# The first stage of a two-layer encoder step, ordered by columns of x instead of by k tiles

## The chip, the cores and the metric

The kernel runs on one core of a Trainium2 chip. The metric is the device time of one execution in microseconds (us). Three runs of the kernel before gave 1068.53, 1067.67 and 1068.82 us, median 1068.53. The kernel is given once with its profile; all times "at" some microsecond below count from the first instruction of the profiled execution. In the text TensorE is also called PE, VectorE DVE, ScalarE ACT, GpSimd POOL and SyncE SP, as the profile names them.

## What is computed

Two layers run over 1024 prompt rows and 64 sample rows (1088 columns in the kernel, which holds everything with features on the partitions). Each layer modulates a normalised input and multiplies it with a wide weight:

```python
cs = jax.nn.silu(c)
for l in range(DEPTH):
    shift, scale, gate = jnp.split(cs @ ada_w[l] + ada_b[l], 3, axis=-1)
    h = _rmsnorm(x, norm_g[l]) * (1 + scale[:, None]) + shift[:, None]
    ... h @ w_in ...
    x = x + gate[:, None] * out
```

This case concerns only the start of layer 0: load x, `h = x * rstd * A + B` with `A = norm_g * (1 + scale)` and `B = shift`, and the first two of the weight tiles of `h @ w_in`. All of it is float32 with exact products: h and each weight are split into a rounded high part and a low rest, and three products (high x high, high x low weight, low h x high weight) are summed.

## The kernel before

x arrives as 8 k tiles of 128 features by 1088 columns. The columns form three chunks (`CHUNKS`: 364, 364 and 360 columns; the last has the prompt's end and all 64 sample columns, so its two parts take different modulation columns). `startup` (L304) does this, with the order of each engine's instructions written out by hand from L367 on (`manual_schedule`: each engine's queue is the program's order):

- SP issues the loads in program order (L308 to L324): 8 tiles of x whole, unit 0 of the modulation weight (2 MiB), k tiles 0 and 1 of two weight tiles W0 and W1, unit 1, their k tiles 2 to 7, units 2 and 3.
- Squares on ScalarE (L329) and their sum over k tiles on VectorE (L331, in `acc`), then per chunk three products with ones on TensorE (`sums`, L383), a power -1/2 on GpSimd (L387), a broadcast by transposes (L395), and a copy back to `acc` by ScalarE (L396): `acc` then holds rstd for every column.
- `ada_steps` (L166 to L184) makes the shift and scale of two k tiles from one unit: 64 records of products on TensorE, a copy of the rows by VectorE (`ada_rows`, L170), a transpose (L173), additions (L179) and A (L184). Unit u gives k tiles 2u and 2u+1. `unit(u)` issues the products and the copy, the rest comes where `all_of(steps)` stands.
- `scale` (L347) multiplies a k tile of x by rstd on VectorE. `h` (L349) then makes two passes of ScalarE (L357): the rounded high part `ah` and the unrounded value `hf`, each in two pieces (prompt and sample columns); VectorE makes `al = hf - ah` (L364).
- `w_split` (L403) makes the high part of the weights on ScalarE (L405) and the low part by a subtraction on GpSimd, or for k tiles 2 to 7 of W1 on VectorE (L407).
- `part(kt, ns, which)` (L334) issues one to three of the products of k tile kt for both weight tiles and all three chunks: 6 products for each of the three kinds, 144 in all, into six PSUM banks `first` that stay open to the end of the stage.

After the stage the six banks are evacuated (L1013), one more modulation unit runs on TensorE and the products of all further weight tiles follow (L269 and others).

## Time and profile before

| | us |
|---|---|
| median of three runs | 1068.53 |
| the profiled execution | 1068.52 |
| span of its instructions | 1066.8 |
| TensorE busy in the span | 1043.7 |
| first product of the stage starts | 26.61 |
| last products of the stage start | 57.25 and after |

The span is the time from the first to the last instruction of the profile; 1.7 us lie around it. A row of the timeline gives start, length, engine, line, operation and tiles (written<-read), shapes and a count; in square brackets stand the idle time of the engine before it and what ended that. Matmuls overlap: six that start 0.167 us apart show as 1.16 us. Windows give busy time of each engine and the granted clock of TensorE (1.00 is 2.4 GHz, 0.50 is 1.2 GHz).

### The profile page before, as it was taken

What the parts mean: (1) busy time and instruction counts of PE and PEld (TensorE: products, weight loads), DVE (VectorE), ACT (ScalarE), POOL (GpSimd) and SP (SyncE); (2) the same over time, 40 slices, a digit from 0 to 9 for tenths busy, and PEclk for the clock granted to TensorE, in tenths of its full rate; (3) what the DMA queues carried; (4) which work ended last, traced back from release to release, by engine and by line L of the source; (5) the groups of instructions that cost most, each with busy time, mean ns of one, the idle gap of its engine ahead of it and who ended that gap; (6) DMA issues with size and microseconds to landing.
All of it is one profiled execution on the core that took longest, in us unless ns stands there. A gap on an engine that the chain in (4) does not pass through costs nothing.

```text
span 1066.8 us, 20069 instructions
## 1 busy us (share of the span) xinstructions
PE 1043.7 (98%) x7535; PEld 1014.4 (95%) x7535; DVE 722.3 (68%) x1854; ACT 591.7 (55%) x1160; POOL 498.9 (47%) x531
## 2 busy tenths in 40 slices
PE   6999999999999999999999999999999999999996
PEld 5999889999999999999999999999999999998996
DVE  5723889888887767677786455885478666776134
ACT  5935776856776697677687233643345343355110
POOL 1124313465576365455366356564346444465221
PEclk9999999999999999999999999999999999999998
DMA  9862521211010120000001712031111311124012
GB/s 362 339 240 96 213 99 61 82 57 43 22 40 25 40 75 21 21 21 19 3 20 42 266 69 100 40 120 40 41 41 31 129 41 60 60 80 158 1 69 99
DMA packets 31008, 90.30 MB, mean 85 GB/s; under 512 B 5568, under 2 KB 11968, under 8 KB 27456
## 3 DMA queue, kind: packets, MB, share of 16 engines
q1 hardware_dynamic: 30912, 89.03, 23.7%
q8 instruction: 59, 0.97, 0.4%
q14 instruction: 37, 0.30, 0.1%
HBM read 78.44 MB, written 10.58 MB: 83 GB/s over the span
## 4 chain that ended last, share of the span: by engine, by line
PE 90%; DVE 4%; ACT 2%; issue 2%; POOL 1%; DMA 0%; POOLq 0%; DVEq 0%; ACTq 0%
PE st L1393 21%; PE pj L269 19%; PE op L269 16%; PE pj L286 14%; PE av L793 3%; PE logit_ps L749 3%; PE p_ps L775 3%; PE ada_ps L167 2%; PE first L342 2%; PE score_ps L485 2%; PE sgu_ps L1461 1%; PE score_ps L486 1%; DVE acc L331 1%; POOL x L1281 1%; PE v_ps L1433 1%
## 5 line engine op out<-in xcount | busy, mean ns | idle before, releaser
L259 POOL TENSOR_TENSOR w_lo<-w_raw,w_hi 128x1024 fp32r<-128x1024 f32 x35 | 84.3, 2408 | 147.2 <-ACT w_hi L258 140.8
L269 PE MATMUL pj<-ah,w_hi 128*128 128x364 f32 (+1 forms) x440 | 145.2, 330 | 0.0
L269 PE MATMUL pj<-al,w_hi 128*128 128x364 f32 (+1 forms) x440 | 144.6, 329 | 0.0
L269 PE MATMUL pj<-ah,w_lo 128*128 128x364 f32 (+1 forms) x440 | 143.3, 329 | 0.0
L1393 PE MATMUL st<-ah,p_w 128*128 128x272 f32 x704 | 137.3, 290 | 0.3 <-ACT ring L1494 0.3
L604 DVE TENSOR_SCALAR_CACHE_REDUCE junk<-S,cand 128x512 bf16<-128x512 f32 (+5 forms) x142 | 119.0, 838 | 2.2
L1393 PEld LDWEIGHTS st<-ah,p_w 128*128 128x128 f32 x704 | 111.7, 188 | 1.4 <-issue 0.7
L286 PE MATMUL pj<-ah,w_lo 128*128 128x364 f32 (+1 forms) x304 | 100.3, 330 | 0.0
L286 PE MATMUL pj<-ah,w_hi 128*128 128x364 f32 (+1 forms) x304 | 100.2, 330 | 0.0
L286 PE MATMUL pj<-al,w_hi 128*128 128x364 f32 (+1 forms) x304 | 100.1, 329 | 0.0
L1360 POOL TENSOR_TENSOR p_w<-p_s,p_w 128x512 fp32r<-128x512 f32 x44 | 58.7, 1337 | 79.4 <-ACT p_w L1359 79.3
L1393 PE MATMUL st<-al,p_w 128*128 128x272 f32 x352 | 93.0, 291 | 0.0
L631 ACT ACTIVATE junk<-S,cand 128x896 bf16<-128x896 f32 (+2 forms) x78 | 77.7, 997 | 26.4 <-DVE m L634 24.5
L1253 DVE SCALAR_TENSOR_TENSOR x<-op,mod,x 128x192 f32<-128x192 f32 (+2 forms) x64 | 30.1, 495 | 91.4 <-PE op L269 87.5
L269 PEld LDWEIGHTS pj<-ah,w_hi 128*128 128x128 f32 x440 | 82.6, 188 | 0.6 <-ACT w_hi L258 0.3
L269 PE MATMUL op<-ah,w 128*128 128x448 f32 (+2 forms) x336 | 82.5, 330 | 0.4 <-DVE u L1420 0.4
L756 POOL TENSOR_SCALAR S<-S,sm 128x128 f32<-128x128 f32 (+8 forms) x68 | 51.6, 763 | 66.6 <-DVE sm L755 55.0
L269 PEld LDWEIGHTS pj<-al,w_hi 128*128 128x128 f32 x440 | 82.7, 188 | 0.1
L269 PEld LDWEIGHTS pj<-ah,w_lo 128*128 128x128 f32 x440 | 82.5, 188 | 0.0
L1393 PEld LDWEIGHTS st<-al,p_w 128*128 128x128 f32 x352 | 66.3, 188 | 0.3 <-issue 0.2
L269 PE MATMUL op<-ah,w_hi 128*128 128x384 f32 (+2 forms) x200 | 65.2, 326 | 0.0
L269 PE MATMUL op<-ah,w_lo 128*128 128x384 f32 (+2 forms) x200 | 65.1, 326 | 0.0
(322 smaller groups left out, 2977.1 us busy)
## 6 DMA issues: line engine op xcount, KB each, us to landing
ada<-in_ada_w SPq DMA_DIRECT2D x21, 1024.0 KB, 7.6
w_raw<-in_w SPq DMA_DIRECT2D x31, 512.0 KB, 3.5
p_raw<-in_w SPq DMA_DIRECT2D x44, 256.0 KB, 2.9
w_raw<-in_wo SPq DMA_DIRECT2D x16, 512.0 KB, 3.5
x<-in_x SPq DMA_DIRECT2D x8, 544.0 KB, 6.0
bo<-in_ada_w SPq DMA_DIRECT2D x2, 1024.0 KB, 6.9
x<-in_x SPq DMA_DIRECT2D x1, 1792.0 KB, 7.6
spill<-x SPq DMA_DIRECT2D x1, 1792.0 KB, 5.7
```

What stands on the lines that cost most here:

```text
L259: (nc.gpsimd if lo_eng == "pool" else nc.vector).tensor_sub(lo, raw, hi)
L269: last = self.nc.tensor.matmul(ps, wt[:, kt, :], at[:, kt, c0:c1], start=n == 0, stop=n == len(mms) - 1)
L286: self.nc.tensor.matmul(ps, wt[:, kt, :], at[:, kt, a:b], start=kt == 0 and i == 0, stop=kt == KT - 1 and i == 2)
L604: V.tensor_scalar(junks[0][:, 0:SW[j]], self.S[:, span(j)], thr, 0.0, op0=OP.is_lt, op1=OP.add, accum_out=col(cv, j))
L631: nc.scalar.activation(junks[1][:, 0:SW[j]], self.S[:, span(j)], AF.Sign, scale=-1.0, bias=col(cand, j), accum_out=col(cv, j))
L749: nc.tensor.matmul(pt[:, 0:w], lhs, keys[i][:, t // 2, s], start=i == 0, stop=i == 1)
L756: self.lastnorm = nc.gpsimd.tensor_scalar(p, p, st[:, 3:4], 0.5, op0=OP.mult, op1=OP.mult).ins
L775: nc.tensor.transpose(pt[0:r, o:o + P], p[:, j * P:j * P + r], self.ident)
L793: self.lastav = nc.tensor.matmul(av[:, 0:m], self.vs[0:r, vbase + j, t // 2, :], part[0:r, x:x + m], start=j == 0 and i == 0, stop=(j + 1) ...
L1253: nc.vector.scalar_tensor_tensor(x[:, t, a:b], ps[:, a:b], self.mod[l][:, 16 + t, j:j + 1], x[:, t, a:b], op0=OP.mult, op1=OP.add)
L1360: nc.gpsimd.tensor_sub(w[:, 1], src, w[:, 0])
L1393: nc.tensor.matmul(ps, w[:, p, k, :], at[:, k, :], start=i == 0, stop=i == len(mms) - 1)
```

## The change

The first stage goes by columns. `C2` is 728, the start of the last chunk. "Front" means columns 0 to 727, "back" 728 to 1087.

- Loads: columns 0 to 727 of all k tiles of x, unit 0, k tiles 0 to 3 of W0 and W1, unit 1, columns 728 to 1087 of all k tiles of x, unit 2, k tiles 4 to 7 of W0 and W1, unit 3. That is 8 loads more.
- Squares, sums and rstd are made for the front first, and for the back later, between other work. The bank `last` takes the sums and the rstd of the back.
- `part` takes the chunks as well, and the products of k tiles 0 to 3 are issued front and back separately. k tiles 4 to 7 are made whole, as before.
- `h` takes one k tile and its spans. For an even k tile it is as before. For an odd one VectorE first does `x = x * A * acc` (scalar_tensor_tensor in the place of `scale`), ScalarE makes `ah = x + B` in one pass, and VectorE makes `al = (x + B) - ah` (scalar_tensor_tensor in the place of the subtraction).
- `w_split` takes both weight tiles, k tiles 0 and 1, then 2 and 3, then 4 to 7; all low parts go to GpSimd.

```diff
         for kt in range(KT):
-            self.load(x[kt], self.i["x"][:, kt, :])
+            self.load(x[kt][:, 0:C2], self.i["x"][:, kt, 0:C2])
...
         for u in range(4):
-            if u in (1, 2):
-                w_load(*((0, 2), (2, KT))[u - 1])
+            if u in (1, 3):
+                k = slice(0, KH) if u == 1 else slice(KH, KT)
+                for n in range(2):
+                    self.load(wraw[n][:, k, :], self.i["w0"][n, :, k, :])
+            if u == 2:
+                for kt in range(KT):
+                    self.load(x[kt][:, C2:TC], self.i["x"][:, kt, C2:TC])
...
+            if kt % 2:
+                for a, b, j in spans:
+                    nc.vector.scalar_tensor_tensor(x[kt][:, a:b], x[kt][:, a:b], mod(A, j), acc[:, a:b],
+                                                   op0=OP.mult, op1=OP.mult)
+                for a, b, j in spans:
+                    nc.scalar.activation(self.ah[:, kt, a:b], x[kt][:, a:b], AF.Identity, bias=mod(B, j))
+                yield
+                for a, b, j in spans:
+                    nc.vector.scalar_tensor_tensor(self.al[:, kt, a:b], x[kt][:, a:b], mod(B, j), self.ah[:, kt, a:b],
+                                                   op0=OP.add, op1=OP.subtract)
...
+            def w_split(a, b):
+                for n in range(2):
+                    nc.scalar.activation(ws[n][0][:, a:b, :], wraw[n][:, a:b, :], AF.Copy)
+                    nc.gpsimd.tensor_sub(ws[n][1][:, a:b, :], wraw[n][:, a:b, :], ws[n][0][:, a:b, :])
...
+            scale(0, CHUNKS[:2])
+            all_of(early)
+            w_split(0, 2)
+            warm(7, WARM[2])
+            late = [h(0, front), h(1, front)]
+            next(late[0])
+            next(late[1])
             for some in late:
                 all_of(some)
+            w_split(2, KH)
+            scale(2, front)
+            F, B = (0, 1), (2,)
+            part(0, (0, 1), cs=F)
+            part(1, (0, 1), cs=F)
+            part(0, (2,), cs=F)
+
+            for kt in range(3):
+                square(kt, ((C2, TC),), "sq2", TC - C2)
+            steps = unit(1)
+            part(1, (2,), cs=F)
+            for kt in range(3, 5):
+                square(kt, ((C2, TC),), "sq2", TC - C2)
+            all_of(steps)
+            for kt in range(5, KT):
+                square(kt, ((C2, TC),), "sq2", TC - C2)
+            r = sums(2, last, TC - C2)
+            late = [h(2, front), h(3, front)]
+            next(late[0])
+            next(late[1])
+            part(2, (0, 1), cs=F)
+            rstd(2, r, last)
+
+            scale(0, back)
+            all_of(late[0])
+            late0 = h(0, back)
+            next(late0)
+            all_of(late[1])
+            part(3, (0, 1), cs=F)
+            part(2, (2,), cs=F)
+            steps = unit(2)
+            part(3, (2,), cs=F)
+            all_of(late0)
+            part(0, (0, 1), cs=B)
+            late1 = h(1, back)
+            next(late1)
+            scale(2, back)
+            late2 = h(2, back)
+            next(late2)
+            all_of(steps)
+            all_of(late1)
+            w_split(KH, KT)
+            part(1, (0, 1), cs=B)
+            scale(4, both)
+            late4 = h(4, both)
+            next(late4)
+            all_of(late2)
+            part(2, (0, 1), cs=B)
+            all_of(h(3, back))
+            for kt in range(2):
+                part(kt, (2,), cs=B)
+            part(3, (0, 1), cs=B)
+            for kt in range(2, 4):
+                part(kt, (2,), cs=B)
+            steps = unit(3)
+            part(4, (0, 1))
+            all_of(late4)
+            late5 = h(5, both)
+            next(late5)
+            all_of(steps)
+            scale(6, both)
+            late6 = h(6, both)
+            next(late6)
+            all_of(late5)
+            part(5, (0, 1))
+            part(4, (2,))
```

## Rows read from the trace of the kernel before

**Rows 1.** The page: TensorE's share of the span, and the chain's by engine.
```profile
PE 1043.7 (98%) x7535; PEld 1014.4 (95%) x7535; DVE 722.3 (68%) x1854; ACT 591.7 (55%) x1160; POOL 498.9 (47%) x531
...
PE 90%; DVE 4%; ACT 2%; issue 2%; POOL 1%; DMA 0%; POOLq 0%; DVEq 0%; ACTq 0%
```

**Rows 2.** Windows, four stretches of the span; the header names the columns.
```profile
core 0: us, PE busy (x) PEld busy (x) DVE busy (x) ACT busy (x) POOL busy (x), PEclk, DMA share, GB/s
0.00:8.40 8.40, 0.00 (x0) 0.03 (x1) 0.51 (x4) 4.92 (x6) 0.90 (x7) 1.00 0.78 257
8.40:26.60 18.20, 16.92 (x124) 13.51 (x125) 13.08 (x20) 9.87 (x15) 3.96 (x5) 0.91 1.02 409
26.60:57.60 31.00, 30.58 (x338) 28.59 (x337) 21.48 (x28) 24.72 (x35) 2.97 (x1) 1.00 0.85 322
57.60:1066.80 1009.20, 996.20 (x7077) 972.28 (x7076) 687.24 (x1803) 552.24 (x1106) 491.10 (x518) 1.00 0.20 70
```

**Rows 3.** The chain that ended last, from 0 to 27 us: start, length, what.
```profile
0.80 3.91 DMA x<-in_x
...
15.39 1.30 DVE acc L331
...
16.79 0.55 DVE acc L331
...
17.38 2.17 PE sums L383 x18
```

**Rows 4.** Groups by line and form, 0 to 58 us: busy, mean ns of one, idle before.
```profile
L357 ACT ACTIVATE hf<-x,mod,modA 128x1024 f32<-128x1024 f32 x8 | 9.9, 1234 | 0.0
L347 DVE TENSOR_TENSOR x<-x,acc 128x1088 f32<-128x1088 f32 x7 | 8.9, 1284 | 0.0
...
L331 DVE TENSOR_TENSOR acc<-acc,sq 128x1088 f32<-128x1088 f32 x6 | 7.8, 1292 | 7.5 <-ACT sq L329 7.0
...
L329 ACT ACTIVATE sq<-x 128x1088 f32<-128x1088 f32 x6 | 6.6, 1109 | 1.2 <-DVE acc L331 1.2
...
L357 ACT ACTIVATE hf<-x,mod,modA 128x64 f32<-128x64 f32 x8 | 3.4, 430 | 0.0
...
L387 POOL TENSOR_TENSOR rs<-rs,nhalf 128x3 f32<-128x3 f32 x3 | 2.5, 855 | 16.5 <-DVE rs L386 16.5
...
L405 ACT ACTIVATE w_hi<-w_raw 128x768 fp32r<-128x768 f32 x2 | 1.6, 835 | 0.0
...
L347 DVE TENSOR_TENSOR x<-x,acc 128x364 f32<-128x364 f32 x2 | 1.1, 540 | 2.6 <-ACT acc L396 2.5
```

**Rows 5.** Timeline of TensorE, 16 to 60 us.
```profile
26.61 1.69 PE L342 MATMUL first<-ah,w_hi 128*128 128x364 f32 x6
...
34.40 1.95 PE L167 MATMUL ada_ps<-ada,cs 128*32 128x128 f32 x64
...
39.48 1.16 PE L342 MATMUL first<-ah,w_hi 128*128 128x364 f32 x6
...
51.15 1.27 PE L342 MATMUL first<-al,w_hi 128*128 128x364 f32 x6 [0.34 <-DVE al L364]
...
57.25 1.16 PE L342 MATMUL first<-al,w_hi 128*128 128x364 f32 x6
```

**Rows 6.** Timeline of VectorE, 15 to 60 us.
```profile
44.59 0.29 DVE L170 COPY ada_rows<-ada_ps 128x128 f32<-128x128 f32 x1 [1.67 <-PE ada_ps L167]
45.85 0.23 DVE L179 TENSOR_TENSOR mod<-ada_ps,adab 128x4 f32<-128x4 f32 x2 [0.97 <-PE ada_ps L173]
```

**Rows 7.** Groups by line and form of VectorE, 1040 to 1066 us.
```profile
L1289 DVE SCALAR_TENSOR_TENSOR x<-x,fg,rstd 128x384 f32<-128x384 f32 x8 | 4.3, 607 | 0.4 <-PE rstd L238 0.4
```

**Rows 8.** Windows, two finer stretches; columns as in rows 2.
```profile
17.38:20.13 2.75, 2.75 (x42) 2.73 (x46) 1.32 (x5) 0.00 (x0) 1.63 (x2) 1.00 1.06 406
20.13:23.55 3.42, 3.42 (x40) 2.66 (x36) 1.13 (x3) 1.50 (x4) 0.88 (x2) 0.50 1.03 422
```

More of the change, by code (lines that the diff above doesn't have):

```diff
@@ L307, in startup @@
         x = [sp.tile([P, TC], F32, name=f"x{kt}") for kt in range(KT)]
+        C2 = CHUNKS[2][0]
+        front, back, both = ((0, C2, 0),), ((C2, SEQ, 0), (SEQ, TC, 1)), ((0, SEQ, 0), (SEQ, TC, 1))
         for kt in range(KT):
-            self.load(x[kt], self.i["x"][:, kt, :])
+            self.load(x[kt][:, 0:C2], self.i["x"][:, kt, 0:C2])
             if kt < 5:
@@ new lines, in h, with mod @@
+        def h(kt, spans):
+            def mod(m, j):
+                return m[:, kt, j:j + 1]
+            A, B = self.modA[0], self.mod[0]
+            if kt % 2:
[8 more added lines that the diff above has]
+                                                   op0=OP.add, op1=OP.subtract)
+            else:
+                if kt not in hf:
+                    hf[kt] = sp.tile([P, TC], F32, tag="hf0", name="hf0", bufs=2)
+                for i, out in enumerate((self.ah[:, kt, :], hf[kt])):
+                    for a, b, j in spans:
+                        for c, d in ((a, CHUNKS[0][1]), (CHUNKS[1][0], b)) if kt + i + a == 0 else ((a, b),):
+                            nc.scalar.activation(out[:, c:d], x[kt][:, c:d], AF.Identity, scale=mod(A, j),
+                                                 bias=mod(B, j))
+                yield
+                s = slice(spans[0][0], spans[-1][1])
+                nc.vector.tensor_sub(self.al[:, kt, s], hf[kt][:, s], self.ah[:, kt, s])
@@ L373, in warm, with sums, rstd, all_of @@
                     nc.tensor.matmul(pt[:, 0:256], self.ident, x[kt][:, 0:256], start=True, stop=True)
+            def sums(c, pt, o0):
+                a, b = CHUNKS[c]
+                n = len(pieces(b - a))
+                for j, o in enumerate(pieces(b - a)):
+                    nc.tensor.matmul(pt[:, o0 + j:o0 + j + 1], acc[:, a + o:a + o + P], self.ones,
+                                     start=True, stop=True)
+                r = self.small.tile([P, 4], F32, tag="rs", name="rs", bufs=3)
+                nc.vector.tensor_scalar(r[:, 0:n], pt[:, o0:o0 + n], 1.0 / D, EPS, op0=OP.mult, op1=OP.add)
+                nc.gpsimd.tensor_tensor(r[:, 0:n], r[:, 0:n], self.nhalf[:, 0:n], op=OP.pow)
+                return r
+            def rstd(c, r, rb):
+                a, b = CHUNKS[c]
+                for j, o in enumerate(pieces(b - a)):
+                    nc.tensor.transpose(rb[:, o:o + P], r[:, j:j + 1].to_broadcast([P, P]), self.ident)
+                nc.scalar.activation(acc[:, a:b], rb[:, 0:b - a], AF.Copy)
+            def all_of(steps):
+                for _ in steps:
+                    pass
             warm(2, WARM[0])
             warm(7, WARM[1])
[L378 to L388 removed]
+            rs = [sums(c, self.bank("pj", "sums"), 0) for c in range(2)]
             early = self.ada_steps(0, 0, lambda kt: raws[0][:, kt, :])
@@ new lines, in startup @@
+            part(3, (0, 1), cs=B)
[13 more added lines that the diff above has]
+            part(4, (2,))
+            late7 = h(7, both)
+            next(late7)
```

105 lines of the change are left out of this document (22 added, 83 removed).

## The prediction

> **What bounds the kernel now.** I read the page first: TensorE is busy in 98% of the span and holds 90% of the chain [rows 1]. The windows then tell the start from the rest. After 57.6 us TensorE is busy in 996 of 1009 us, so a shift of the first stage's end reaches the end of the program almost whole. Between 26.6 and 57.6, the stretch in which the change works, it is busy 30.58 of 31.0 us, while VectorE has 21.5 and ScalarE 24.7 us of work [rows 2]. The largest wait of TensorE in there is 0.34 us [rows 5]. Ahead of it lies a chain without TensorE work of use: eight tiles of x arrive, VectorE adds their squares one after another, 17.3 us are gone when the last sum starts, and the first product comes at 26.61 [rows 3, 5]. So there are two things to weigh: how much sooner the first product can start, and whether the stage behind it stays free of holes.
>
> **How I work it out.** I go through the queues of TensorE, VectorE, ScalarE and GpSimd in the program's order. An instruction starts when its engine is free and its inputs are there (0.04 us after the producer's end, 0.1 us where an addition follows one on the same columns: starts are 1.40 us apart for additions of 1.29 [rows 3, 4]). Lengths are scaled by columns between the forms in the rows. VectorE: 0.54 us for 364 and 1.28 for 1088 columns, so 0.91 for 728 and 0.53 for 360. ScalarE: 1.23 and 0.43 us for the two pieces of a pass, of which each hides 0.1 under the next, so a pass is 1.47 us and its back part 0.86 [rows 4]. TensorE: 0.167 us a product, 1.9 us a unit [rows 5]. The same procedure on the order of before gives 25.9 us for the first product and some 57 us for the end, each up to 1 us under the rows, so I only use differences between the two walks.
>
> **The start: 5.4 us sooner.** A tile of x has 364 instead of 544 KB; at 409 GB/s it takes 0.9 instead of 1.4 us [rows 2], and a square and an addition shrink alike. Seven additions 1.02 us apart from about 7.2 us on put the end of the first chunk's sum at 13.9 us, where before it is at 17.3 [rows 3]. 12 instead of 18 sums, and two powers instead of three at 0.86 us each [rows 4], end at 17.0. Unit 0 arrives 1.47 MB / 409 GB/s = 3.6 us sooner, so its last products run at about 17.4, A is there at 19.7 and the first product at 20.5, against 25.9 in the walk of before.
>
> **New TensorE work: +1.0 us.** The sums and transposes of the last chunk move from the front, where TensorE waited anyway, into the stage: six records at 0.112 us and three transposes at 0.107.
>
> **New holes: +10.9 us.** This is what decides. The products of a front k tile are 2.0 us instead of 3.0, while ScalarE and VectorE still serve each k tile in order and now make the back as well.
> - *Front, 0.9 us.* Products of k tile 1 wait for its ScalarE pass, queued behind both passes of k tile 0.
> - *The sums of the back, 2.95 us (27.4 to 30.3).* TensorE has done the front of k tiles 0 and 1 and unit 1 by 27.4; next in its queue stand the back's sums. VectorE, after the front's low parts and `scale(2)`, reaches the back's additions at 25.7. Seven of them at 0.63 us, with unit 1's row copy and three small modulation steps written between them, end at 30.3. The last back tile lands before that: 9.2 MB are ahead of its end, which [rows 2] give as 25.6 us, and 28 with the lag between rate and landing; were it 29.3, 0.9 us more.
> - *Four small ones, 2.1 us.* Behind those sums TensorE waits for the high part of k tile 3 (VectorE's multiplication stands behind the power's input), the low part of k tile 2, and the back of k tiles 1 and 2.
> - *The back of k tile 3, 4.2 us (42.0 to 46.2).* VectorE's copy of unit 2's rows stands ahead of the back's low part and of the multiplication of k tile 1, so ScalarE idles until 39.0. Then it has, in order, the back of 1 (0.8), of 2 (1.8), two weight parts (1.1), both passes of k tile 4 (2.9) and only then the back of 3 (0.8): 46.2. TensorE has 3.8 us of products in this time, and unit 3 stands behind the back of 3. Such a copy waits for its unit in the trace as well [rows 6], but there ScalarE has passes ahead.
> - *After unit 3, 2.0 us (51.5 to 53.5).* The unit ends at 49.4. VectorE then copies its rows, makes the low part of k tile 4 (1.3) and the multiplication of 5 (1.4), ScalarE its pass (1.2): 53.5. TensorE has only the 2.0 us of k tile 4 in between.
>
> Together 12.3 us of holes, of which the walk of before has 1.4. **The sum so far** is -5.4 + 1.0 + 10.9 = +6.5 us.
>
> **The terms without a row.** A ScalarE pass with a bias tile alone is not in the trace: the square, with neither tile, takes 1.11 us for 1088 columns, while 1024 columns with both take 1.23 [rows 4], an overhead of 0.1 to 0.28 us on the start-to-start time. With these ends the sum is 5.8 and 7.1; I take 0.2, the middle. scalar_tensor_tensor takes 0.61 us for 384 columns [rows 7] where the plain form would take 0.56 by the column rate: between nothing and 0.05 each, or 0 to +0.15 us of the sum; I take nothing. The eight added loads and the later refill of the weight slots cost nothing by the queue: the next tile's weight would land near 49 us, and is used only after the stage; were the cover gone, that is one load.
>
> **The clock, +1.7 us.** TensorE's granted clock is 1.2 GHz from 20.13 to 23.55 after a stretch in which it did little but one-column sums and part of a unit, and 2.4 GHz in the busy stretches around [rows 8, 2]. The hole of 4.2 us has no product at all. I expect a stretch as long as that one at 1.2 GHz behind it, which holds 1.7 us less work, while the back of 3 and unit 3 are on the path. The term is between 0 and 1.7 us for this hole; the hole of 2.95 us would add 1.1 in the same way (less, since part of the work behind it waits for VectorE anyway). The Trainium skill, "TensorE: Matmul & The Clock Gate", section "What's actually happening", says the slow clock is the default and activity releases it. This speaks against the change: by it the sum is +8.2 us or more, and with a clock that holds through the hole +6.5.
>
> The forecast is +8.2 us on the profiled execution's 1068.52 us, which is the median of the three runs (1068.53): **1076.7 us**.
>
> **Rivals.**
> - *The clock holds: 1075.0.* For it: nothing in the rows shows an idle hole in mid-stage. Against it: rows 8.
> - *Both holes lower it: 1077.8.*
> - *The back arrives late: 1079.7.* Its rows of 1440 bytes may move slower than the 409 GB/s of [rows 2]; every us beyond 28 delays the sums and all behind them. Three us more give this.
> - *ScalarE gets ahead: 1070.8.* If VectorE reaches the multiplication of k tile 1 before TensorE needs it, the 4.2 us hole closes and its clock loss with it: 6.5 - 4.2 = +2.3.
> - *No change, 1067.8.* The 2.95 us hole closes too: -0.7.
> - *Faster: 1064.1.* VectorE and ScalarE keep ahead of TensorE throughout, so that the early start stays and only the 1.4 us of holes of before remain: -5.4 + 1.0 = -4.4. For it speaks that by sums of work both are below TensorE in the stage [rows 2], and ScalarE loses four passes of 1.47 us. It holds as soon as holes come to less than 5.8 us in all; against it stands the order of the row copies, which makes VectorE wait for TensorE, and TensorE then for VectorE.
> - *The change doesn't do what it says* has no case of its own: loads and order are plain in the diff.
>
> **How the numbers follow.** Chances: forecast 0.33, clock holds 0.20, both holes 0.12, late back 0.08, ScalarE ahead 0.08, no change 0.06, faster 0.13. A measurement of this kernel can tell some 0.2% (2.1 us) from no change. Slower: 0.33 + 0.20 + 0.12 + 0.08 + 0.08 = 0.81; within: 0.06; faster: 0.13. The range from 1070.8 to 1079.7 takes in these five cases and the bounds (+5.8, and 7.1 + 0.9 + 2.8 = +10.8), and leaves out 0.19.
>
> **What the profile after would show.** Right: the first product near 21 us; a TensorE wait of about 3 us on an addition of VectorE before the sums of the back; one of about 4 us on ScalarE's high part before the back of k tile 3, with ScalarE in the passes of k tile 4 just before; one of 2 us after unit 3; a granted clock of 0.50 after the second; the stage's last products near 66 us. Wrong: a stage after 26 us without waits of over 1 us, or a first product that is no earlier. A shift of the stage's end that isn't found again in the span would put the cause behind the stage, where I expect none.

## The result and the profile after

The changed kernel takes 1078.88 us (median of four runs, 1078.03 to 1079.32), the kernel before 1068.35 (median of four too). The ratio is 1.0098 with a 95% interval of 1.0081 to 1.0116: slower by 10.5 us. The profiled execution of the changed kernel is the one of 1079.32 us; its span is 1077.5.

The page of the changed kernel, its busy times and the chain by engine, as in [rows 1]:

```profile
PE 1047.0 (97%) x7535; PEld 1016.3 (94%) x7535; DVE 729.9 (68%) x1878; ACT 587.9 (55%) x1166; POOL 499.6 (46%) x534
...
PE 92%; DVE 3%; ACT 2%; issue 1%; DMA 0%; POOL 0%; SPq 0%; POOLq 0%; DVEq 0%; ACTq 0%
```

It says next to nothing: shares of a span of 1077 us move by a point when 10 us go. The windows say where, in the changed kernel (columns as in [rows 2]):

```profile
8.40:26.60 18.20, 16.89 (x131) 13.80 (x131) 11.05 (x19) 9.85 (x18) 4.60 (x6) 1.00 1.02 387
26.60:57.60 31.00, 23.06 (x271) 19.62 (x270) 19.36 (x42) 15.38 (x30) 5.55 (x4) 0.89 0.68 261
...
68.84:1077.50 1008.66, 995.63 (x7073) 971.78 (x7072) 690.77 (x1803) 551.08 (x1105) 488.60 (x518) 1.00 0.20 71
```

Between 26.6 and 57.6 us TensorE is busy for 23.06 us instead of 30.58 [rows 2], at a mean granted clock of 0.89 instead of 1.00. VectorE and ScalarE too are busy for less of this stretch than before (19.36 instead of 21.48 and 15.38 instead of 24.72 us), so no engine is full: all three stand idle in turn. (It isn't less work in all: the stage now runs past 57.6, and over the span VectorE has 7.6 us more and ScalarE 3.8 us less.) Behind the stage nothing changes: from its next unit to the end of the span there are 1008.66 us, in the kernel before 1008.46 (1066.8 less the start of that unit, below).

TensorE's timeline in the changed kernel, the rows with waits and those that mark the stage (start, length; in brackets the idle time ahead and what ended it):

```profile
16.11 1.40 PE L399 MATMUL sums<-ones,acc 128*128 128x1 f32 x12
...
22.75 1.01 PE L349 MATMUL first<-ah,w_hi 128*128 128x364 f32 x4
...
24.84 0.93 PE L349 MATMUL first<-ah,w_hi 128*128 128x364 f32 x4 [0.42 <-ACT ah L369]
...
32.53 0.83 PE L399 MATMUL rstd<-ones,acc 128*128 128x1 f32 x6 [2.58 <-DVE acc L336]
...
38.33 0.92 PE L349 MATMUL first<-al,w_hi 128*128 128x364 f32 x4 [0.31 <-DVE al L384]
...
43.24 0.60 PE L349 MATMUL first<-ah,w_hi 128*128 128x360 f32 x2 [0.48 <-ACT ah L369]
...
49.59 0.60 PE L349 MATMUL first<-ah,w_hi 128*128 128x360 f32 x2 [3.92 <-ACT ah L369]
...
51.40 3.24 PE L167 MATMUL ada_ps<-ada,cs 128*32 128x128 f32 x64
...
58.64 1.27 PE L349 MATMUL first<-ah,w_hi 128*128 128x364 f32 x6 [1.70 <-ACT ah L369]
...
68.84 1.08 PE L167 MATMUL ada_ps<-ada,cs 128*32 128x128 f32 x32
```

Two rows of TensorE in the kernel before, its products that warm TensorE up and the unit that answers to the last row above:

```profile
8.40 8.60 PE L373 MATMUL warm<-x,ident 128*128 128x256 f32 x26 [8.40 <-DMA x<-in_x]
...
58.34 1.08 PE L167 MATMUL ada_ps<-ada,cs 128*32 128x128 f32 x32
```

So the stage's end moves from 58.34 to 68.84, +10.5 us, and that is the whole result. It splits at the first product: 26.61 [rows 5] to 22.75, 3.86 us sooner; from there to the next unit 46.09 us instead of 31.73, 14.36 longer. Of these, waits of TensorE are 0.42 + 2.58 + 0.31 + 0.48 + 3.92 + 1.70 = 9.41 us, where before has 0.34 [rows 5].

Unit 3 (51.40) takes 3.24 us instead of 1.95 [rows 5]. The windows of the changed kernel, cut where its granted clock changes, show why:

```profile
13.13:33.61 20.48, 16.60 (x199) 13.77 (x199) 12.79 (x28) 11.54 (x22) 5.80 (x6) 1.00 1.02 392
33.61:37.03 3.42, 3.42 (x15) 3.33 (x14) 1.01 (x2) 1.38 (x2) 1.51 (x1) 0.50 1.03 413
37.03:50.68 13.65, 8.94 (x101) 7.40 (x101) 10.04 (x22) 8.96 (x18) 2.83 (x2) 1.00 0.31 108
50.68:54.09 3.41, 3.41 (x55) 2.81 (x58) 0.00 (x0) 0.00 (x0) 0.00 (x0) 0.50 0.99 390
54.09:70.00 15.91, 14.19 (x126) 13.20 (x118) 9.94 (x16) 7.60 (x12) 0.03 (x1) 1.00 0.63 230
```

One stretch at 1.2 GHz (0.50) follows the wait of 2.58 us, another the wait of 3.92. Each holds half the work of its length, 1.7 us less. The stretch of before at 0.50, in the front [rows 8], is gone.

### The profile page after: what moved, and what is told of

Its sections match the earlier page's. It is cut to its first block, busy times and chain, and to the rows that moved or that the text cites. A ratio compares the mean times of both kernels' runs of the same rounds, so it can differ in the third digit from the quotient of the medians.

```text
span 1077.5 us, 20120 instructions
## 1 busy us (share of the span) xinstructions
PE 1047.0 (97%) x7535; PEld 1016.3 (94%) x7535; DVE 729.9 (68%) x1878; ACT 587.9 (55%) x1166; POOL 499.6 (46%) x534
## 4 chain that ended last, share of the span: by engine, by line
PE 92%; DVE 3%; ACT 2%; issue 1%; DMA 0%; POOL 0%; SPq 0%; POOLq 0%; DVEq 0%; ACTq 0%
PE st L1465 21%; PE pj L269 20%; PE op L269 16%; PE pj L286 14%; PE av L865 3%; PE logit_ps L821 3%; PE p_ps L847 3%; PE ada_ps L167 2%; PE first L349 2%; PE score_ps L557 2%; PE sgu_ps L1533 1%; PE score_ps L558 1%; PE warm L393 1%; PE v_ps L1505 1%; PE op L1304 0%
## 5 line engine op out<-in xcount | busy, mean ns | idle before, releaser
L1432 POOL TENSOR_TENSOR p_w<-p_raw,p_w 128x512 fp32r<-128x512 f32 x33 | 46.8, 1420 | 39.8 <-ACT p_w L1431 38.1
```

Of the source, the lines that this page charges most:

```text
L1432: nc.gpsimd.tensor_sub(w[:, 1], src, w[:, 0])
```

## The experiments

The theory: the order of the instructions in the queues of ScalarE and VectorE makes TensorE wait, and the clock falls behind the two long waits. The rivals: the waits have another owner (the arrival of the back), the work doesn't fit whatever its order, or the new form of the odd k tiles is itself to blame. The table gives each kernel's median, its ratio to runs of the kernel before on the same chip, and from its profile the first product, the time from there to the next unit, and in between the waits of TensorE and the time at a granted clock of 0.50 (1.2 GHz).

| kernel | median us | ratio, 95% interval | first product | to next unit | waits in it | at clock 0.50 |
|---|---|---|---|---|---|---|
| before | 1068.35 | 1 | 26.61 | 31.73 | 0.34 | 0 |
| changed | 1078.88 | 1.0081 to 1.0116 | 22.75 | 46.09 | 9.41 | 6.83 |
| e2_h3_first | 1076.47 | 1.0065 to 1.0095 | 21.01 | 44.14 | 7.24 | 6.83 |
| e3_pad | 1076.40 | 1.0060 to 1.0094 | 22.25 | 43.93 | 4.56 | 0 |
| e4_copy_late | 1078.07 | 1.0081 to 1.0111 | 22.53 | 44.49 | 7.73 | 6.83 |
| e5_warm6 | 1078.66 | 1.0090 to 1.0120 | 20.98 | 47.08 | 9.61 | 10.24 |
| e6_back_order | 1076.41 | 1.0062 to 1.0092 | 20.85 | 44.46 | 6.38 | 10.24 |
| e7_front_order | 1080.37 | 1.0096 to 1.0132 | 22.35 | 47.11 | 9.04 | 10.24 |
| e8_all_order | 1077.22 | 1.0071 to 1.0101 | 22.26 | 44.13 | 6.28 | 10.24 |
| e9_columns_alone | 1081.28 | 1.0104 to 1.0132 | 21.91 | 49.26 | 10.53 | 13.66 |
| e10_best_order | 1071.52 | 1.0014 to 1.0034 | 20.66 | 39.80 | 3.44 | 0 |
| e1_odd_alone | 1070.46 | 1.0013 to 1.0032 | 27.30 | 33.68 | 2.08 | 0 |
| e11_odd_ahead | 1071.13 | 1.0011 to 1.0029 | 27.29 | 33.72 | 1.86 | 0 |
| e12_odd_low_ahead | 1067.95 | 0.9988 to 1.0007 | 25.18 | 31.38 | 0.25 | 0 |

The profiles say which wait goes and which comes; the medians say what is left of it. (The first product differs by up to 1.9 us among kernels whose code is the same up to there; the section on the steps comes back to that.) The kernels ran on several chips, and the median of the kernel before was between 1067.54 and 1068.56 there, so a difference of 1 us between two medians of the table is not resolved.

The last column matters as much as the waits. A stretch at 0.50 came out 3.4 us long behind some waits and 6.8 behind others, so that several kernels with shorter waits lose more to the clock than the changed kernel: 6.8 us at 0.50 are up to 3.4 us less work, 10.2 up to 5.1 (less where TensorE waits inside the stretch). There is one profile of each kernel; how much of this belongs to the kernel and how much to the execution is not shown.

### The wait before the back of k tile 3

What stands in ScalarE's queue in the changed kernel just before that pass, by its timeline:

```profile
44.81 1.14 ACT L436 ACTIVATE w_hi<-w_raw 128x512 fp32r<-128x512 f32 x2
45.85 1.56 ACT L380 ACTIVATE ah<-x,mod,modA 128x1024 fp32r<-128x1024 f32 x2
47.31 1.56 ACT L380 ACTIVATE hf<-x,mod,modA 128x1024 f32<-128x1024 f32 x2
48.78 0.76 ACT L369 ACTIVATE ah<-x,mod 128x296 fp32r<-128x296 f32 x2
```

Weight parts, both passes of k tile 4, then the pass that TensorE needs. The first experiment, e2_h3_first, moves it:

```diff
             all_of(late1)
+            late3 = h(3, back)
+            next(late3)
             w_split(KH, KT)
...
-            all_of(h(3, back))
+            all_of(late3)
```

> The changed kernel, with the multiplication and the ScalarE pass of k tile 3's back moved ahead of the last weight parts and of k tile 4. Theory (the order of ScalarE's queue makes TensorE's wait of 3.92 us before the back of k tile 3, and the half clock behind it follows from it): ScalarE's three passes ahead of it (1.56 + 1.56 and the weight parts) fall behind, the wait shrinks to under 1 us, the stretch at 0.50 after 50.7 us goes, and the time falls by 4 to 5.5 us, to some 1074. Rival A (VectorE, or the arrival of the back, is what TensorE really waits for there): the wait stays at over 3 us and the time within 1 us. Rival B (the gain comes back as a wait for k tile 4, which now stands later on ScalarE): the 3.9 us hole goes, one of 2 to 3 us opens behind unit 3, and the time falls by under 2 us.

Measured: 1076.47 us, 2.4 less than the changed kernel. The wait before the high part is gone and with it the stretch at 0.50 behind it, but a wait of 2.08 us has come in another place. TensorE, VectorE and GpSimd in this run:

```profile
48.50 0.60 PE L349 MATMUL first<-al,w_hi 128*128 128x360 f32 x2 [2.08 <-DVE al L372]
...
45.69 2.75 DVE L372 SCALAR_TENSOR_TENSOR al<-x,mod,ah 128x296 fp32r<-128x296 f32 x2
...
45.56 2.80 POOL L437 TENSOR_TENSOR w_lo<-w_raw,w_hi 128x512 fp32r<-128x512 f32 x2 [11.37 <-ACT w_hi L436]
```

The theory's place was right, its size was not. Of rival A the arrival of the back falls, since the loads are unchanged and the wait went. VectorE as a second owner doesn't fall: the edit moves the multiplication on VectorE as well as the pass on ScalarE, and in the changed kernel that multiplication ended only 0.35 us before ScalarE came to the pass (the section on the steps has the rows). Beside the new wait, the half-clock stretch behind the sums is twice as long here, from 30.5 to 37.4 us, so the clock costs as much as in the changed kernel:

```profile
30.20:37.03 6.83, 6.08 (x23) 6.00 (x24) 2.46 (x7) 3.42 (x5) 1.52 (x1) 0.53 1.02 401
```
Next in line behind the high part is the low part, a fused instruction of VectorE in two pieces that takes 2.75 us while GpSimd subtracts weights, from 45.56 to 48.36.

e6_back_order takes GpSimd away from there and puts the low part ahead of k tile 4:

```diff
             all_of(late[1])
+            w_split(KH, KT, nc.vector)
             part(3, (0, 1), cs=F)
...
-            w_split(KH, KT)
             part(1, (0, 1), cs=B)
+            late3 = h(3, back)
+            next(late3)
+            all_of(late2)
+            all_of(late3)
             scale(4, both)
```

> The changed kernel, with all of k tile 3's back ahead of k tile 4 (as in the run that moved its pass), its low part too, and with the last weight parts made earlier, after k tile 0's back, the low ones on VectorE instead of GpSimd. Theory (when its pass came sooner, TensorE next waited 2.08 us for the low part of k tile 3, because that fused instruction of VectorE took 2.75 instead of 1.3 us beside GpSimd's weight subtraction): with nothing on GpSimd there and the low part ahead of k tile 4, the waits between 42 and 50 us come to under 1 us; the time falls by some 4.5 to 5.5 us against the changed kernel, to about 1074, and by 2 us against the run that moved the pass alone. Rival (VectorE simply has more work than fits there, GpSimd or not): the wait moves to k tile 4 or to the low parts, the sum of the waits stays above 2 us, and the time stays within 0.7 us of 1076.5.

Measured: 1076.41 us, no better than e2_h3_first. VectorE, TensorE and ScalarE in it:

```profile
44.91 0.71 DVE L372 SCALAR_TENSOR_TENSOR al<-x,mod,ah 128x296 fp32r<-128x296 f32 x2
...
53.58 1.76 PE L349 MATMUL first<-ah,w_hi 128*128 128x364 f32 x6 [2.69 <-ACT ah L369]
...
46.79 1.57 ACT L380 ACTIVATE ah<-x,mod,modA 128x1024 fp32r<-128x1024 f32 x2 [1.70 <-DVE x L354]
```

Without GpSimd beside it the same low part takes 0.71 us, so that step of the theory holds: between 42 and 50 us only 0.48 us of waits are left. But the wait behind unit 3 has grown from 1.69 to 2.69 us: k tile 4's passes now start at 46.79, since its multiplication is what was put behind. The time is the rival's. Its reason, that VectorE has too much work, is only a part: the waits fell by 3.0 us in sum, but TensorE ran at 0.50 for 10.24 us instead of 6.83, which takes up to 1.7 us of that back. A wait that was closed here showed up at the next instruction of the same engine.

### The wait behind unit 3

Two rows of VectorE in the changed kernel, the copy of unit 3's rows and the multiplication behind it:

```profile
54.72 0.29 DVE L170 COPY ada_rows<-ada_ps 128x128 f32<-128x128 f32 x1 [4.66 <-PE ada_ps L167]
...
56.13 1.47 DVE L366 SCALAR_TENSOR_TENSOR x<-x,modA,acc 128x1024 f32<-128x1024 f32 x2
```

VectorE stands still for 4.66 us with work behind the copy. e4_copy_late:

```diff
-            steps = unit(3)
-            part(4, (0, 1))
             all_of(late4)
             late5 = h(5, both)
             next(late5)
+            steps = unit(3)
+            part(4, (0, 1))
```

> The changed kernel, with the low part of k tile 4 and the multiplication of k tile 5 ahead of the copy of unit 3's rows in VectorE's queue. Theory (the 1.70 us wait behind unit 3 comes from that copy, which waits 4.66 us for TensorE's unit with VectorE's work queued behind it): the wait for the high part of k tile 5 goes and the time falls by 1.4 to 2 us, to some 1077. Rival (ScalarE's passes, or the multiplications themselves, set it): the wait stays above 1 us, and the time changes by under 0.5 us.

Measured: the wait of 1.70 us is gone and the stage is 1.60 us shorter (44.49), as expected; the median, 1078.07 (1077.12 to 1079.06), is 0.8 us lower, and its range overlaps that of the changed kernel. The cause is shown by the profile, the size in the time is not resolved.

### The clock

e3_pad fills the two long waits with products that nobody uses, 5 ahead of the sums of the back and 8 ahead of the back of k tile 3:

```diff
+            def pad(n):
+                for _ in range(n):
+                    nc.tensor.matmul(last[:, 0:256], self.ident, x[7][:, 0:256], start=True, stop=True)
```

> The changed kernel, with products that nobody uses (256 columns, identity by x) put into two of TensorE's waits: 5 before the sums of the back, 8 before the back of k tile 3. Everything else is unchanged, and the waits keep their ends, which other engines set. Theory (each hole drops the granted clock to 0.50 for a stretch behind it, and that costs 1.2 to 1.7 us beside the hole itself): with TensorE kept busy the clock stays at 1.00 from 13 us on, and the time falls by 2.8 to 3.2 us. Rival A (only the holes cost, the work at the half clock hides beside VectorE's and ScalarE's work): the clock stays up and the time stays within 0.7 us. Rival B (the clock falls for another reason than the holes): the two stretches at 0.50 are there again, and the time is the same or, by the products that are added, up to 1 us longer.

Measured: 1076.40 us, 2.5 less, with nothing but useless work added. Its windows:

```profile
12.41:33.00 20.59, 18.89 (x210) 15.66 (x210) 12.76 (x28) 11.57 (x22) 5.79 (x6) 1.00 1.02 392
33.00:57.60 24.60, 20.86 (x219) 17.84 (x218) 16.68 (x34) 12.85 (x24) 4.37 (x3) 1.00 0.59 224
```

The clock stays at 2.4 GHz throughout, and the stretch to the next unit is 2.16 us shorter. That is a little under the 2.8 expected: TensorE, faster now, meets small waits that weren't there (0.42 us for the power's result, 0.70 instead of 0.31 before k tile 2's low part). Rivals A and B fall.

### The start

e5_warm6 asks for 6 instead of 10 of the first products that warm TensorE up.

```diff
-WARM = (10, 3, 3)
+WARM = (6, 3, 3)
```

> The changed kernel, with 6 instead of 10 of the products that warm TensorE up on the tile of k tile 2. Theory (the first product came at 22.75 and not 5.4 us earlier than before because these products, at the half clock until 13.13 us, still ran when the sum of the squares was done at 14.4, so that the sums started at 16.1): with four fewer the sums start near 14.5, the first product near 21.2, and the time falls by 1 to 1.7 us if the clock rises as before. Rival A (the first product waits for the unit's weights or the powers, not for the sums): the first product stays within 0.3 us of 22.75 and the time with it. Rival B (the clock rises later or falls once more, since TensorE does less): the sums start earlier but unit 0 runs at 0.50 in part, the first product gains under 0.7 us, and the time is the same or longer.

Measured: the sums start at 14.22 instead of 16.11 and the first product comes at 20.98, 1.77 sooner; but the median is 1078.66, only 0.2 less. The stage is 0.99 us longer (the clock is at 0.50 for 10.24 us instead of 6.83, the second stretch now from within the wait of 3.91 us to 53.0), and what remains in the profile, 0.8 us, is not resolved in the medians. The theory is right about the first product; that the gain reaches the end is not shown.

### The sums of the back

e7_front_order puts k tile 2's and 3's front ahead of the last three additions (`sq_act` and `sq_add` are the square and the addition by themselves); its core:

```diff
-            for kt in range(5, KT):
-                square(kt, ((C2, TC),), "sq2", TC - C2)
-            r = sums(2, last, TC - C2)
             late = [h(2, front), h(3, front)]
             next(late[0])
+            sq_add()
+            sq_act(7)
+            sq_add()
+            next(late[1])
             part(2, (0, 1), cs=F)
+            sq_add()
+            all_of(late[0])
+            r = sums(2, last, TC - C2)
```

> The changed kernel, with k tile 2's and 3's front ahead of the last of the eight squares and additions of the back, and their products ahead of or around the back's sums. The loads are unchanged. Theory (the 2.58 us wait before the sums is TensorE standing in line behind VectorE's additions while it had products to do): TensorE starts k tile 2 some 1.5 us earlier, its waits between 28 and 38 us fall from 3.3 to 1.8 us or less, and the time falls by 1 to 1.5 us, more by up to 1.4 if the clock no longer falls there. Rival A (the arrival of the back sets it): the additions' end stays where it was and something behind the sums waits instead: k tile 0's back; the time is within 0.7 us. Rival B (the modulation of unit 1 is not there sooner): the wait stands before k tile 2 instead, unchanged in size.

Measured: 1080.37 us, no gain; the median is 1.5 more than the changed kernel's, but the runs of the two overlap. Its TensorE:

```profile
31.48 0.93 PE L349 MATMUL first<-ah,w_hi 128*128 128x364 f32 x4 [1.94 <-ACT ah L380]
...
38.42 0.84 PE L410 MATMUL rstd<-ident,rs 128*128 128x128 f32 x3
...
50.36 0.97 PE L349 MATMUL first<-ah,w_hi 128*128 128x360 f32 x2 [3.90 <-ACT ah L369]
```

k tile 2 starts 1.74 us sooner (31.48 instead of 33.22), but the transposes of the back's rstd come 2.96 us later (38.42 instead of 35.46), and k tile 3's back still waits 3.90 us. The waits are 0.4 us less in sum, but behind the sums the clock is at 0.50 from 33.2 to 40.0 us, 6.8 instead of 3.4, and that alone costs 1.7 us. Neither the theory nor a rival had a longer stretch at 0.50 in it.

e8_all_order does this and the reorderings of e6_back_order and e4_copy_late together.

> The changed kernel with all three reorderings together: the last squares behind k tile 2's and 3's front, k tile 3's back and the weight parts ahead of k tile 4, the low part of 4 and the multiplication of 5 ahead of unit 3's row copy, the low part's products of 4 ahead of k tile 5's. No work is added or taken away. Theory (holes are 9.1 us of the stage's 14.4 us growth and the clock behind them some 3): waits of TensorE between the first product and the next unit fall from 9.4 to under 4 us, and the time to 1068 to 1071. Rival A (the work of VectorE and ScalarE doesn't fit any order): the waits stay above 6 us in sum, and the time above 1074. Rival B (the loss lies to a good part elsewhere, in shorter products and half-clock stretches): the waits fall below 4 us, but the time stays above 1072.

Measured: 1077.22 us, waits of 6.28 us, the rival's outcome: that particular order hits TensorE twice at a unit's transposes (1.57 and 1.01 us), because VectorE's copy of the rows now stands behind other work. This is that order's outcome, not proof that none fits: e10_best_order, below, leaves less.

### The two parts of the change by themselves

e1_odd_alone takes the kernel before and makes only the odd k tiles the new way (`mul` is the multiplication by A and rstd on VectorE; their low parts are fused as in the change):

```diff
+                if kt % 2:
+                    mul(kt)
+                    for a, b, j in both:
+                        nc.scalar.activation(self.ah[:, kt, a:b], x[kt][:, a:b], AF.Identity,
+                                             bias=self.mod[0][:, kt, j:j + 1])
+                    continue
```

> The kernel before, in which only the odd k tiles of h are made the new way (a multiplication by A and rstd together on VectorE, one pass of ScalarE with the bias, a fused addition and subtraction for the low part); loads, squares, sums and the order of products stay as before. Theory (the loss lies in the cutting by columns and its order, not in this): TensorE sets the stage of before, whose largest wait was 0.34 us, so four passes of 1.5 us less on ScalarE bring nothing; within 1 us of before, 1067.5 to 1069.5. Rival A (the new odd k tiles cost, since VectorE's fused form of 1.47 us stands ahead of ScalarE's pass and the low part waits for it): waits of TensorE before odd k tiles, 2 us or more over before. Rival B (they help): 1 to 2 us under before, by a first product that comes sooner.

Measured: 1070.46 us, 0.13% to 0.32% over before. Rival A was right. TensorE and VectorE in this run:

```profile
41.45 1.26 PE L342 MATMUL first<-ah,w_hi 128*128 128x364 f32 x6 [0.91 <-ACT ah L366]
...
37.32 0.29 DVE L170 COPY ada_rows<-ada_ps 128x128 f32<-128x128 f32 x1 [1.09 <-PE ada_ps L167]
38.58 0.23 DVE L179 TENSOR_TENSOR mod<-ada_ps,adab 128x4 f32<-128x4 f32 x2 [0.97 <-PE ada_ps L173]
38.85 0.16 DVE L184 SCALAR_TENSOR_TENSOR modA<-mod,ng 128x4 f32<-128x4 f32 x1
38.93 1.48 DVE L354 SCALAR_TENSOR_TENSOR x<-x,modA,acc 128x1024 f32<-128x1024 f32 x2
```

k tile 3's A is there at 34.0, but its multiplication stands behind unit 2's row copy and modulation steps and starts at 38.93. The old multiplication needed no A and had been made two k tiles ahead. e11_odd_ahead moves it in front of the copy's steps:

```diff
-                    all_of(steps)
-                    all_of(h((2 * u, 2 * u + 1)))
+                    late = h((2 * u, 2 * u + 1))
+                    next(late)
                     part(2 * u, which=(0, 1))
+                    all_of(steps)
+                    all_of(late)
```

> The kernel in which only the odd k tiles are made the new way, with the multiplication and the pass of each odd k tile moved ahead of the next unit's row copy in VectorE's queue (and that unit's transposes behind the products of the even k tile). Theory (there TensorE waited twice 0.91 us for the high part of an odd k tile, since its multiplication, which now needs A, stands behind the row copy and the modulation steps of the next unit, while the old pass of ScalarE stood behind neither): both waits go, and the time falls by 1.5 to 2 us, to that of before within 1 us. Rival (the fused multiplication and the single pass are simply longer on the way, 1.48 + 1.39 us behind each other): waits of 0.5 us or more stay before the odd k tiles, and the time falls by under 0.7 us.

Measured: 1071.13 us. The two waits are gone, and two of 0.93 us have come before the even low parts; VectorE in it:

```profile
40.35 0.23 DVE L179 TENSOR_TENSOR mod<-ada_ps,adab 128x4 f32<-128x4 f32 x2 [1.58 <-PE ada_ps L173]
...
41.90 1.29 DVE L379 TENSOR_TENSOR al<-hf,ah 128x1088 fp32r<-128x1088 f32 x1
```

That looked like the rival, but VectorE idles for 1.58 us just ahead, with that low part queued behind. e12_odd_low_ahead adds one line, the low part ahead of the modulation steps:

```diff
                     part(2 * u, which=(0, 1))
+                    next(late)
                     all_of(steps)
```

> The kernel in which only the odd k tiles are made the new way and each odd multiplication stands ahead of the next unit's row copy's modulation steps, now with the low part of the even k tile (and the next even multiplication) ahead of these modulation steps too. Theory (in the run before TensorE's two waits of 0.93 us came from VectorE, which idled 1.58 us in front of the modulation steps with the even low part queued behind them; the new form of the odd k tiles costs nothing by itself): both waits go, the stretch from the first product to the next unit is 31.8 us or less, as before the change, and the time is within 1.2 us of before. Rival (VectorE's chain of a fused multiplication, a multiplication and two low parts between two units is too long in any order): a wait of 0.5 us or more per unit remains, in front of a low part or of the modulation, and the time stays 1.5 us or more above before.

Measured: 1067.95 us, ratio 0.9998 (0.9988 to 1.0007). The stretch to the next unit is 31.38 us with one wait of 0.25, shorter than before's 31.73. So the new form of the odd k tiles costs nothing here; two places in VectorE's queue cost 2 to 3 us. It brings nothing either: TensorE sets the stage. (The first product at 25.18 in this profile goes with a front without the stretch at 0.50 that the kernel before has [rows 8]; the medians show no gain.)

e9_columns_alone is the other half, the cutting by columns with the old odd k tiles:

> The changed kernel, whose odd k tiles are made the old way again (multiplication by rstd on VectorE, two passes of ScalarE with A and B, a plain subtraction); the cutting by columns and its order stay, and the multiplication stands where the fused one stood. Theory (with the odd k tiles alone at +2.3 to +2.9 us over before, the rest of the 10.5 us is the cutting by columns, and ScalarE's second pass of odd k tiles stands mostly where that engine idled): 1077 to 1080, within 1.5 us of the changed kernel. Rival A (the two parts add up): some 2.5 us less than the changed kernel, near 1076.3. Rival B (the second passes, 1.0 us each for a front, go before what TensorE waits for, so the single pass is what the cutting needs): 2 to 4 us more than the changed kernel.

Measured: 1081.28 us, 2.4 over the changed kernel: rival B. Its waits before high parts are longer than the changed kernel's, or new (0.51, 0.60, 0.78, 4.10, 1.73). They make up 1.1 us; the rest goes with the clock, which is at 0.50 for 13.66 us instead of 6.83. So the cutting by columns is the whole loss (+12.7 us alone), and the single pass gives a part of it back. The size of that part is rough: the ratios to the kernel before, 1.0118 and 1.0098, have intervals that overlap.

### All of it together

e10_best_order is e6_back_order with the start of e5_warm6, five of the unused products before the back's sums, and k tile 5's multiplication ahead of unit 3's copy and of k tile 4's low part.

> The changed kernel with what the runs so far pointed to, together: 6 instead of 10 products at the start, 5 unused products before the sums of the back, k tile 3's back and the last weight parts ahead of k tile 4 with the low weight parts on VectorE, and k tile 5's multiplication ahead of unit 3's row copy and of k tile 4's low part. Theory (each of these removes a wait or a half-clock stretch that was on TensorE's path: 1.5 at the start, 1.5 to 2.5 of clock, 3.9 and 1.7 to 2.7 of waits): first product near 21, waits behind it under 2.5 us in sum, and a time of 1069 to 1071.5, at par with before or up to 0.3% over it. Rival (each hole that is closed comes back in another place, as when the front alone was reordered): the waits stay above 5 us in sum and the time above 1074. It would be faster than before only if the sums of the back were there without a wait too.

Measured: 1071.52 us (eight runs), ratio 1.0024 (1.0014 to 1.0034): 7.4 us less than the changed kernel. Its window, from 12 us to the end of the stretch of [rows 2]:

```profile
12.00:57.60 45.60, 40.96 (x437) 34.94 (x438) 33.19 (x69) 28.21 (x51) 7.25 (x7) 1.00 0.84 325
```

and TensorE's longest waits in the stage (sum in us, how many, the longest):

```profile
PE first L349 <- DVE al L372: 0.9, 1, 0.9
PE first L349 <- ACT ah L369: 0.9, 2, 0.5
PE first L349 <- DVE al L384: 0.7, 1, 0.7
```

The clock stays up, waits are 3.44 us, the first product comes at 20.66. The theory holds for the clock, the start and, at its edge, the time (1069 to 1071.5); the waits are over its 2.5 us, and a further 2.3 us of waiting are filled with unused products. This is not the same work in another order alone: the low parts of the last weights are made by VectorE instead of GpSimd, four products at the start are left out and five unused ones added. So the 7.4 us are what order, clock and start give together; the clock alone gave some 2.5 of them in e3_pad. It is still 0.24% over before, as expected without an earlier sum of the back: 39.80 us to the next unit, of which 31.4 are the work of before without its wait, 1.1 the sums and transposes that were moved in, 3.4 waits and 2.3 the unused products in what was a wait; 1.6 us are not named by this.

## Why the prediction was right, step by step

The forecast was 1076.7 us (1070.8 to 1079.7), slower with 0.81. The time is 1078.88, in the range and 2.2 over the forecast. By number the nearest rival is *the back arrives late* (1079.7), but the profile shows no late back (below). By mechanism it is *both holes lower the clock* (1077.8). The direction and its causes are as forecast; that the number is as near as it is, is in part luck, since the terms miss by more than the sum and holes that were smaller make up for a start that gained less:

| term | forecast us | in the profile us |
|---|---|---|
| start | -5.4 | -3.86 |
| new TensorE work | +1.0 | +1.1 (six sums 0.83, three transposes 0.3 at the full clock, as in e3_pad) |
| new holes | +10.9 | +9.1 (9.41 less 0.34) |
| clock | +1.7 | +3.4 (two stretches of 1.7) |
| not accounted for | 0 | +0.8 |
| sum | +8.2 | +10.5 |

(The five holes that the prediction lists add up to 12.15 us, not to the 12.3 that it goes on with, and its steps from 39.0 give 46.4, not 46.2. Neither slip changes the forecast by more than 0.2 us.)

**The start** is the mis-sized term. The step that failed is "end at 17.0" for the powers: in the walk TensorE started the first sums as soon as VectorE's additions were done, near 14. In the trace they start at 16.11, because TensorE was still at the products that warm it up. These products and two windows of the changed kernel:

```profile
7.13 9.14 PE L393 MATMUL warm<-x,ident 128*128 128x256 f32 x26 [7.13 <-DMA x<-in_x]
...
7.13:13.13 6.00, 6.00 (x14) 4.83 (x15) 4.80 (x6) 4.19 (x7) 0.00 (x0) 1.00 1.02 356
13.13:16.11 2.98, 2.92 (x14) 2.22 (x14) 1.69 (x3) 0.65 (x2) 0.00 (x0) 1.00 1.00 412
```

14 records of these products lie in the 6.00 us up to 13.13 and 14 in the 2.98 after it (two of the 26 reach into both): the first ones ran at the half clock. (The window gives 1.00 there too, which doesn't fit these lengths; I go by the lengths.) In the kernel before the same products were done at 17.0 (8.40 and 8.60 us long), ahead of the first sum at 17.38 [rows 3], so they cost nothing there, and the walk put them at nothing. It need not have: the same 8.60 us from an arrival of the tile three times 0.45 us sooner, at 7.05, end at 15.65 by the rows, well behind 13.9. Where the clock happened to rise sooner, in the profiles of e2_h3_first and e6_back_order, or with four of them fewer, in e5_warm6, the first product came at 21.01, 20.85 and 20.98, which is 5.6 to 5.8 us sooner than before, where 5.4 were forecast. It is the cover of the old order that was left out: sums that come sooner meet work that had always been hidden.

**The holes** were found one by one: forecast 0.9, 2.95, 2.1 for the four small ones, 4.2 and 2.0; measured 0.42, 2.58, 0.79 (two of the four are there), 3.92 and 1.70. Places are as the prediction named them, and so is the chain: VectorE stands 2.04 us in front of unit 2's row copy, and ScalarE 3.23 us for the multiplication behind it. From there to the end of the pass of k tile 3's back ScalarE takes 7.1 us, in the walk 7.2. The runs that moved a few instructions each (e2_h3_first, e4_copy_late) bear the places out. What the prediction didn't see is GpSimd. Rows of VectorE, ScalarE and GpSimd in the changed kernel:

```profile
41.20 0.29 DVE L170 COPY ada_rows<-ada_ps 128x128 f32<-128x128 f32 x1 [2.04 <-PE ada_ps L167]
...
42.41 0.78 ACT L369 ACTIVATE ah<-x,mod 128x296 fp32r<-128x296 f32 x2 [3.23 <-DVE x L366]
...
45.69 2.74 DVE L366 SCALAR_TENSOR_TENSOR x<-x,modA,acc 128x296 f32<-128x296 f32 x2
...
45.51 2.83 POOL L437 TENSOR_TENSOR w_lo<-w_raw,w_hi 128x512 fp32r<-128x512 f32 x2 [10.36 <-ACT w_hi L436]
```

k tile 3's multiplication takes 2.74 us beside the weight subtraction and ends at 48.43, 0.35 us before ScalarE comes to its pass (48.78). So two causes end almost together: with only ScalarE's queue taken away and VectorE and GpSimd as they are, the pass could have started 0.35 us sooner, and with only VectorE's multiplication sooner, not at all. That is read from the rows; no run moves the one without the other.

**The clock** fell behind both waits, where I had taken one and called the other a rival at 0.12. The reason I gave for the smaller chance, that the work behind the sums partly waits for VectorE anyway, has something in it: e3_pad brings 2.2 us of the stage back and not 3.4. The sentence of the Trainium skill ("TensorE: Matmul & The Clock Gate", section "What's actually happening"), by which activity is what releases the slow clock, agrees with e3_pad: unused products alone kept the granted clock at 1.00.

**Late arrival of the back** (0.08): no. VectorE's seven additions run back to back in the changed kernel but for the row copy and the modulation steps, and ScalarE's squares wait 1.7 us for VectorE and 0.26 for the loads, before the first of them:

```profile
25.66 0.51 ACT L334 ACTIVATE acc<-x 128x360 f32<-128x360 f32 x1 [0.26 <-DMA x<-in_x]
```

**ScalarE ahead, no change, faster**: the walk's order decided against them. e10_best_order gets 7.4 of the 10.5 us back, by order, clock and start together; how much is order alone is not shown. Even it is not faster, so the rival *faster* would have needed more than these changes, by its rows an earlier sum of the back above all.

**Odd k tiles**: that the single pass helps, or costs at most its overhead, could not be read from before. In the changed kernel it helps by some 2.4 us (e9_columns_alone against it); in the order of before it cost 2 to 3 us until two instructions were moved (e1_odd_alone, e12_odd_low_ahead).

What stays open: the 0.8 us that the table does not account for, how much of e4_copy_late's 1.6 us is in the time, and why a stretch at 0.50 is 3.4 us long in one profile and 6.8 in another.

## What to carry to other kernels

In this kernel, work that was cut finer left each engine less to do while another caught up. Before such a cut, walk the queues and ask of every copy that waits for TensorE what is queued behind it, and put what doesn't depend on it ahead. Where one queue sets the end, taking one wait away can show the next instruction of the same queue, so reorder the whole stretch and look again, rather than add up single gains. A hole in TensorE's work is to be priced with the half-clock stretch that follows it, and an earlier start with the work that the old start had hidden.

## What the runs showed of the hardware

- Unused products in a wait of TensorE paid: 2.5 us less in the median, 2.2 us in the profile, for 13 products that nobody uses (e3_pad).
- The fused instruction of VectorE on 360 columns took 0.71 us alone and 2.75 us beside a subtraction on GpSimd of 2.80 us (e2_h3_first against e6_back_order). The Trainium skill, "SBUF — State Buffer", section "Who interferes with whom", says that the two engines share a pair of ports under an exclusive lock, and that a VectorE instruction with two inputs in SBUF contends with a GpSimd instruction that reads SBUF. The two pieces here agree with it: 1.54 and 1.28 us long, each ended shortly after one of GpSimd's two subtractions.
- TensorE's first rise to 2.4 GHz, told by the lengths of its first products, came at another moment in each execution: 6.0 us after the first product in the changed kernel, while all 26 of them took 9.14 us there and 7.84 in e2_h3_first. With the arrival of x (the first product started between 6.67 and 7.94 us) it moved the first product of the stage between 20.85 and 22.75 us in kernels that are the same up to there, a spread of 1.9 us before any change counts.
- The stretch at 1.2 GHz behind a wait of TensorE was 3.4 us long in some profiles and 6.8 in others, 1.7 or 3.4 us of lost work if TensorE has work throughout.
